# A two-layer attention trunk: the low parts of the mix weights come from an accumulating transfer instead of a VectorE subtraction

## The chip, the cores and the metric

One core of a Trainium2 chip runs the kernel. The metric is the device time of one execution in microseconds. A change counts as faster or slower when the time moves by more than 2%, which here is 13 us.

## The reference, cut to what matters

Two layers over 256 tokens of 1024 features. Each layer normalises, projects, runs three attention branches, gates each branch's product with `w_branch` by a sigmoid of its own mix columns, and projects the sum:

```
h = rmsnorm(x, norm_g)
proj = h @ w_in                       # ..., and 3 * 1024 mix columns at the end
ys = stack([ya, yb, ym])              # three branches, 512 wide each
up = einsum('bsnw,nwd->bsnd', ys, w_branch)
gates = sigmoid(mix.reshape(b, s, 3, 1024))
x = x + sum(gates * up, axis=2) @ w_out
```

Everything is float32. The kernel computes each float32 product as three products of rounded parts: a weight w is cut into a high part (`hi`, w rounded to the type float32r) and a low part (`lo` = w - `hi`), and the activations likewise.

## The kernel before, in words

Weights arrive in units. A unit is one transfer of up to 128 x 1024 floats from HBM into a tile `raw`, issued by SyncE (SP); ScalarE then copies `raw` into `whi` (line 102, shown as CAST), VectorE subtracts `whi` from `raw` into `wlo` (line 103), and TensorE multiplies. Units of the mix weights (`w_mix`) and of the branch weights (`w_br`) are 128 x 768, 384 KB. `mm3` (lines 106 to 108) issues three matmuls for a product: high by high, one with the activations' low part, one with the weights' low part. A mix unit and a branch unit have 18 matmuls each, of 256 columns; six of the 18 read `wlo`.

The tiles `raw`, `whi` and `wlo` have four buffers each, so a unit's parts can be written only after TensorE has finished with the unit four before it.

The order in each layer: memory branch, branch A, branch B (attention between `bq`, `bk`, `bv`), then the mix columns in eight groups j of 128 columns for the three branches. `mixes(j)` takes four mix units; the loop over j runs mixes three groups ahead, so its order is 16 mix units, then by turns two branch units and four mix units, then the last eight branch units, then `w_out`. For each j VectorE multiplies the gates into the branch products (line 543), GpSimd adds the three (lines 545 and 546), and ScalarE and VectorE split the sum (lines 547 and 548). A scheduler orders every engine's instructions by a model of its own; with it, matmuls of the first 16 mix units stand between those of branch B's attention. Each engine then runs its instructions in that order.

```python
def split(hi, lo, src):
    nc.scalar.copy(hi, src)
    nc.vector.tensor_sub(lo, src, hi.bitcast(F32))
```

Of the kernel before, what the change touches and what calls it, by code (L numbers as in the profile page):

```python
# [7 lines left out]
F32 = mybir.dt.float32  # L8
# [5 lines left out]
P = 128  # L14
D = 1024
S = 256
# [8 lines left out]
MS = 128 ** -0.5  # L25
RAW = 4  # units of weights on their way
WARM = 10  # products on zeros that wake the tensor engine's clock while the first loads are under way
WS = (64 ** -0.5) * (8 ** -0.5)

# columns of w_in, in groups of 512  # L30
A_Q, A_K, A_V, A_G, B_Q, B_K, B_V, B_G, M_Q, M_G = range(10)
# [3 lines left out]
def trunk(ctx, tc, x, x_t, mem, mem_t, consts, norm_g, gains, w_grp, w_idx, w_mix, w_kv, w_br, w_o, final_g, out):  # L35
# [13 lines left out]
    def two(tag="big"):  # L49
        """a tile for the high and the low parts: [P, 2, 1024]"""  # L50
        return big.tile([P, 2, 1024], F32R, tag="big", name=tag)
# [26 lines left out]
    def unit(src, n, pieces=1):  # L78
# [11 lines left out]
        return hi, lo  # L90

    newest = []
    between = []

    def load_after(dst, src):
        """a load that waits for the newest unit, so that it doesn't hold up the units before it"""
        nc.gpsimd.tensor_copy(dst.rearrange("p a b -> p (a b)")[:, 0:1] if len(dst.shape) > 2 else dst[:, 0:1],
                              newest[0][:, 0:1].bitcast(F32))
        nc.sync.dma_start(dst, src)
# [19 lines left out]
    def transpose_to(dst_fn, src, t):  # L119
        """[P, 1024] -> 8 blocks [128, P]; dst_fn(c, psum [P, 4, 128])"""  # L120
        for c in range(2):
            pt = bank(pst, "pt")
            for i in range(4):
                nc.tensor.transpose(pt[:, i * P:(i + 1) * P], src[:, (4 * c + i) * P:(4 * c + i + 1) * P], ident)
            dst_fn(c, pt.rearrange("p (a b) -> p a b", b=P))

    def rstd_row(rows, rs):
        """1 / rms of the tokens: on partitions in rs, and in a row, the same on all partitions"""
        pt = bank(pst, "pt")
        for t in range(NT):  # L130
            rstd_of(rows[t], wk.tile([P, D], F32, tag="h", name="sq", bufs=3), rs[t])
            diag = wk.tile([P, P], F32, tag="yf", name="diag")
            nc.vector.tensor_scalar(diag, ident, rs[t], None, op0=ALU.mult)
            nc.tensor.matmul(pt[:, t * P:(t + 1) * P], ones, diag, start=t == 0, stop=True, skip_group_check=True)
        return pt[:, :S]
# [4 lines left out]
    def mem_prep(l, mh, ml, ks):  # L140
        """mem but for 1 / rms, with features on partitions"""
        for k in ks:
            g = gm[:, 1, l, k:k + 1]
            nc.scalar.activation(mh[:, k, :], memT[:, k, :], AF.Copy, scale=g)
            nc.vector.scalar_tensor_tensor(ml[:, k, :], memT[:, k, :], g, mh[:, k, :].bitcast(F32),
                                           op0=ALU.mult, op1=ALU.subtract)
# [13 lines left out]
    def rows_first(wsrc, xh, xl, parts, n, done, ahead=lambda u: None, pools=None, first=False):  # L160
        """tokens on partitions: out[t][:, part] = x @ w, w [P, KC, n]"""
        pools = pools or [(pmm, "mm")] * NT
        acc = [[bank(*pools[t]) for _ in parts] for t in range(NT)]
        step = 2 if n <= 512 else 1
        for u in range(KC // step):
            ahead(u)
            hi, lo = unit(wsrc[:, step * u:step * (u + 1), :], step * n, 2 if first and u == 0 else 1)
            for kk in range(step):
                k = step * u + kk
                for t in range(NT):  # L170
                    for i, (a, b) in enumerate(parts):
                        mm3(acc[t][i][:, :b - a], xh[:, k, t * P:(t + 1) * P], xl[:, k, t * P:(t + 1) * P],
                            hi[:, kk * n + a:kk * n + b], lo[:, kk * n + a:kk * n + b], k == 0, k == KC - 1)
        for t in range(NT):
            for i in range(len(parts)):
                done(t, i, acc[t][i])

    def cols_first(wsrc, xh, xl, nt, done, ahead=lambda u: None):
        """columns on partitions: out[c] = (x @ w).T, w [P, KC, nt * 128]; done(pair of tiles, psum)"""
        n = nt * P  # L180
        acc = [bank(pmm, "mm") for _ in range((nt + 1) // 2)]
        step = 2
        for u in range(KC // step):
            ahead(u)
            hi, lo = unit(wsrc[:, step * u:step * (u + 1), :], step * n)
            for kk in range(step):
                k = step * u + kk
                for c in range(nt):
                    o = acc[c // 2][:, (c % 2) * S:(c % 2 + 1) * S]
                    w0 = kk * n + c * P  # L190
                    mm3(o, hi[:, w0:w0 + P], lo[:, w0:w0 + P], xh[:, k, :], xl[:, k, :],
                        k == 0 and c % 2 == 0, k == KC - 1)
        for c in range((nt + 1) // 2):
            done(c, acc[c])

    def rope(t, ps, dst, nh):
        """dst [P, nh, 64] = rope of psum [P, nh, 64]"""
        cb = cosv[t][:, None, :].to_broadcast([P, nh, 16])
# [10 lines left out]
    def heads_T(qf, dst):  # L209
        """qf[t] [P, 512] -> dst [P, 2, (pair, token)], heads on partitions"""  # L210
        for c in range(2):
            pt = bank(pst, "pt")
            for i in range(2):
                for t in range(NT):
                    j = 2 * c + i
                    nc.tensor.transpose(pt[:, i * S + t * P:i * S + (t + 1) * P], qf[t][:, j * P:(j + 1) * P], ident)  # L216
            split(dst[:, 0, c * 512:(c + 1) * 512], dst[:, 1, c * 512:(c + 1) * 512], pt)
# [11 lines left out]
    def values(l, g, hh, hl, name):  # L229
        """[P, token tile, (head, part, 64)]: the high part first for even heads, last for odd ones, so that it  # L230
        meets the rows of y that the head has"""
        v = two(name)
# [9 lines left out]
    def gate(l, g, hh, hl, s2):  # L242
        """s2 [P, 4, S] = 2 silu(h @ w).T"""
        def done(c, ps):
# [5 lines left out]
    def probs(t, nk, tm, nb, scale=-1.0):  # L250
        """softmax rows of scale * tm, whose maximum is -nb"""
        pr = wk.tile([P, 2, S], F32, tag="pr", name="pr", bufs=4)
# [10 lines left out]
    def pair_scores(p, qT, kT, at):  # L263
        """both heads of a pair, each on its half of the rows and in its own bank: queries of the first tile
        meet the high and the low parts of their 128 keys side by side, those of the second tile all keys"""
        scs = [bank(psa, "sc").rearrange("p (a b) -> p a b", b=S) for _ in range(2)]
# [29 lines left out]
    def attn_out(p, prs, v, y, s2):  # L296
# [13 lines left out]
        for i, pool in enumerate(((psa, "sc"), (pst, "pt"))):  # L310
            # high and low parts of v on rows; the low parts of the second queries' later keys in columns of their own
            yp = bank(*pool)
# [58 lines left out]
    def index_mask(l, hh, hl):  # L371
        """additive masks of the keys that each query picks"""
        qb = wk.tile([P, NT, 512], F32, tag="h", name="qf", bufs=3)
# [38 lines left out]
        def turn(t, r):  # L412
            """one turn of a query tile: takes the 8 largest that are left, the earlier of equals first"""
            nk = P * (t + 1)
# [15 lines left out]
    def normed_first(xT):  # L430
        """of x that is laid out with features on partitions"""
        hh = big.tile([P, KC, S], F32R, tag="big", name="hh")
# [22 lines left out]
    for l in range(L):  # L455
# [54 lines left out]
        def mixes(j):  # L510
            """tanh(mix / 2).T of columns j of the branches"""
            mx = wk.tile([P, 3, S], F32, tag="mix", name="mx", bufs=5)

            def done(c, ps):
                n = 2 if c == 0 else 1
                nc.scalar.activation(mx[:, 2 * c:2 * c + n, :], ps[:, :n * S].rearrange("p (a b) -> p a b", b=S),  # L516
                                     AF.Tanh, scale=0.5)
            cols_first(w_mix[l, j], hh, hl, 3, done)
            return mx
# [31 lines left out]
        last = 3 if l + 1 == L else 0  # L551
        # pieces of the columns of out, each in its own bank; the last ones small, as nothing runs beside their ends
        cuts = [[(0, 512), (512, 1024)], [(0, 512), (512, 768), (768, 1024)] if last else [(0, 512), (512, 1024)]]
# [52 lines left out]
def _constants():  # L606
    """identity, causal masks, cosines and sines: of the shapes alone"""
    import numpy as np
# [65 lines left out]
```

## Time and profile before

| | us |
|---|---|
| device time, median of 2 runs (647.31 and 647.63) | 647.47 |
| span of the profiled execution, first to last instruction | 645.5 |
| what lies around the span (the difference) | 2.0 |
| TensorE matmuls busy | 632.1 |
| VectorE busy | 468.8 |
| ScalarE busy | 372.6 |
| GpSimd busy | 121.0 |

The two runs differ by 0.05%. The profiled execution's own time is its span and some 2.0 us around it. Matmuls overlap, so TensorE's busy time says when it was supplied, not that each busy microsecond is a matmul's own; how far apart matmuls start says how fast it runs.

### The profile page before, as it was taken

The page shows a single profiled execution, that of the slowest core. Times are in us where ns is not written, and L with a number is a line of the kernel's source. Part 1 is how long each engine was busy: PE and PEld are TensorE (multiplying, and loading weights), DVE is VectorE, ACT ScalarE, POOL GpSimd, SP SyncE. Part 2 cuts the span into 40 slices and gives each one's busy share as a digit, 9 for nine tenths or more (in the row PEclk, how much of TensorE's full clock was granted, in tenths as well). Part 3 has the DMA queues.
Part 4 walks back from the last instruction along what each step waited for, and adds up shares of the span by engine and source line. Part 5 has one row for each costly group of instructions (what it writes and reads, how often), then busy time and mean ns, then how long its engine had stood idle before and what let it go on. Part 6 is the DMA issues. An engine that isn't in the chain of part 4 may idle for free.

```text
span 645.5 us, 12071 instructions
## 1 busy us (share of the span) xinstructions
PE 632.1 (98%) x4446; PEld 583.1 (90%) x4446; DVE 468.8 (73%) x1014; ACT 372.6 (58%) x725; POOL 121.0 (19%) x182
## 2 busy tenths in 40 slices
PE   7999999999999999999999999999999999999995
PEld 4989889878999999999889998897898999999984
DVE  5678799778777778557584678987777786755763
ACT  5857655666656756444464656656565766544442
POOL 1303022023102302126010200401210211221422
PEclk9999999999999999999999999999999999999998
DMA  8967454454444456667655745445444445566641
GB/s 298 360 201 233 150 160 141 156 162 137 111 142 124 125 145 198 195 174 221 214 174 135 264 152 164 134 133 170 151 127 133 131 127 148 171 187 184 206 127 65
DMA packets 35051, 108.64 MB, mean 168 GB/s; under 512 B 4016, under 2 KB 4016, under 8 KB 34992
## 3 DMA queue, kind: packets, MB, share of 16 engines
q1 hardware_dynamic: 34704, 107.35, 54.7%
q8 instruction: 35, 0.57, 0.4%
q10 hardware_dynamic: 288, 0.52, 0.2%
q14 instruction: 24, 0.20, 0.1%
HBM read 106.81 MB, written 1.05 MB: 167 GB/s over the span
## 4 chain that ended last, share of the span: by engine, by line
PE 93%; DMA 3%; DVE 2%; ACT 1%; issue 1%; SPq 0%; POOLq 0%; POOL 0%; ACTq 0%; DVEq 0%
PE mm L106 24%; PE mm L108 24%; PE mm L107 24%; PE sc L271 2%; PE sc L108 2%; PE sc L106 2%; PE sc L107 2%; DMA raw<-in_w_kv 2%; PE sc L275 2%; PE pt L216 1%; PE pt L301 1%; DMA xT<-in_x_t 1%; PE pt L106 1%; PE pt L108 1%; PE pt L107 1%; PE pt L303 1%
## 5 line engine op out<-in xcount | busy, mean ns | idle before, releaser
L103 DVE TENSOR_TENSOR wlo<-raw,whi 128x1024 fp32r<-128x1024 f32 (+3 forms) x225 | 246.9, 1099 | 99.5 <-ACT whi L102 98.5
L102 ACT CAST whi<-raw 128x1024 fp32r<-128x1024 f32 (+3 forms) x225 | 208.1, 927 | 130.3 <-PE mm L107 52.0
L107 PE MATMUL mm<-hl,whi 128*128 128x256 f32 x640 | 183.4, 287 | 0.0
L106 PE MATMUL mm<-hh,whi 128*128 128x256 f32 x640 | 182.9, 286 | 0.0
L108 PE MATMUL mm<-hh,wlo 128*128 128x256 f32 x640 | 182.6, 286 | 0.0
L106 PEld LDWEIGHTS mm<-hh,whi 128*128 128x128 f32 x640 | 122.6, 192 | 1.3
L107 PEld LDWEIGHTS mm<-hl,whi 128*128 128x128 f32 x640 | 122.6, 192 | 0.8
L108 PEld LDWEIGHTS mm<-hh,wlo 128*128 128x128 f32 x640 | 122.4, 192 | 0.7
L108 PE MATMUL mm<-whi,hl 128*128 128x512 f32 (+1 forms) x224 | 84.8, 381 | 1.4 <-DVE hl L103 1.4
L107 PE MATMUL mm<-wlo,hh 128*128 128x512 f32 (+1 forms) x224 | 85.7, 384 | 0.0
L106 PE MATMUL mm<-whi,hh 128*128 128x512 f32 (+1 forms) x224 | 84.2, 380 | 0.0
L260 POOL TENSOR_SCALAR pr<-pr,rinv 128x256 f32<-128x256 f32 (+1 forms) x80 | 40.7, 526 | 183.6 <-DVE rinv L258 175.9
L108 PEld LDWEIGHTS mm<-whi,hl 128*128 128x128 f32 x224 | 42.1, 189 | 8.3 <-DVE hl L103 1.7
L107 PEld LDWEIGHTS mm<-wlo,hh 128*128 128x128 f32 x224 | 42.2, 189 | 7.0
L106 PEld LDWEIGHTS mm<-whi,hh 128*128 128x128 f32 x224 | 41.8, 188 | 7.3
L255 ACT ACTIVATE pr<-tm,nb 128x128 f32<-128x128 f32 (+1 forms) x80 | 36.5, 459 | 9.1 <-DVE nb L291 9.0
L545 POOL TENSOR_TENSOR mx<-mx 128x256 f32<-128x256 f32 x16 | 21.3, 1334 | 102.8 <-DVE mx L543 102.8
L207 POOL TENSOR_TENSOR qf<-rt,rt 128x128 f32<-128x128 f32 (+2 forms) x24 | 16.8, 704 | 121.2 <-DVE rt L206 121.2
L546 POOL TENSOR_TENSOR mx<-mx 128x256 f32<-128x256 f32 x16 | 23.1, 1446 | 12.6 <-DVE mx L543 11.5
L543 DVE SCALAR_TENSOR_TENSOR mx<-mx,mm 128x256 f32<-128x256 f32 x48 | 18.6, 415 | 6.6 <-PE mm L108 6.5
L516 ACT ACTIVATE mx<-mm 128x512 f32<-128x512 f32 (+1 forms) x32 | 15.7, 490 | 12.9 <-PE mm L108 12.9
L547 ACT ACTIVATE mgh<-mx 128x256 fp32r<-128x256 f32 x16 | 6.7, 418 | 25.5 <-POOL mx L546 25.5
(252 smaller groups left out, 1220.9 us busy)
## 6 DMA issues: line engine op xcount, KB each, us to landing
raw<-in_w_grp SPq DMA_DIRECT2D x80, 512.0 KB, 3.9
raw<-in_w_mix SPq DMA_DIRECT2D x64, 384.0 KB, 3.2
raw<-in_w_br SPq DMA_DIRECT2D x32, 384.0 KB, 3.4
raw<-in_w_o SPq DMA_DIRECT2D x16, 512.0 KB, 4.4
raw<-in_w_kv SPq DMA_DIRECT2D x15, 512.0 KB, 4.4
raw<-in_w_idx SPq DMA_DIRECT2D x16, 292.0 KB, 3.1
memT<-in_mem_t SPq DMA_DIRECT2D x4, 256.0 KB, 6.0
xr<-in_x SPq DMA_DIRECT2D x2, 512.0 KB, 6.6
```

The lines of the kernel that those rows point to most:

```text
L102: nc.scalar.copy(hi, src)
L103: nc.vector.tensor_sub(lo, src, hi.bitcast(F32))
L106: nc.tensor.matmul(o, lh, rh, start=start, stop=False, skip_group_check=True)
L107: nc.tensor.matmul(o, lh, rl, start=False, stop=False, skip_group_check=True)
L108: nc.tensor.matmul(o, ll, rh, start=False, stop=stop, skip_group_check=True)
L207: nc.gpsimd.tensor_tensor(dst[:, :, 0:16], t1[:, :nh], t2[:, :nh], op=ALU.add)
L255: nc.scalar.activation(pr[:, i, :nk], tm[:, i, :nk], AF.Exp, bias=nb[:, i:i + 1], scale=scale, accum_out=rsum[:, i:i + 1])
L260: nc.gpsimd.tensor_scalar(pr[:, i, :nk], pr[:, i, :nk], rinv[:, i:i + 1], 1.0, op0=ALU.mult, op1=ALU.mult)
L516: nc.scalar.activation(mx[:, 2 * c:2 * c + n, :], ps[:, :n * S].rearrange("p (a b) -> p a b", b=S), AF.Tanh, scale=0.5)
L543: nc.vector.scalar_tensor_tensor(mt[n], mx[:, n, :], 1.0, ups[n // 2][:, (n % 2) * S:(n % 2 + 1) * S], op0=ALU.add, op1=ALU.mult)
L545: nc.gpsimd.tensor_tensor(mt[0], mt[0], mt[1], op=ALU.add)
L546: nc.gpsimd.tensor_tensor(mt[0], mt[0], mt[2], op=ALU.add)
```

## The change

The mix units, and no others, get their parts in another way (`unit_sum`). ScalarE copies `raw` into `whi` as before, then writes `-whi` into `wlo` by an activation with scale -1; then GpSimd issues a transfer that reads the same 384 KB of `w_mix` from HBM a second time and adds it onto `wlo`. VectorE's subtraction of those units is gone. The sum is the same: `-hi + w`. The other lines of the diff only remove comments, which moves line numbers by up to 14.

```diff
+    def unit_sum(src, n):
+
+        raw = wp.tile([P, 1024], F32, tag="raw", name="raw", bufs=RAW)
+        hi = wp.tile([P, 1024], F32R, tag="whi", name="whi")
+        lo = wp.tile([P, 1024], F32R, tag="wlo", name="wlo")
+        nc.sync.dma_start(raw[:, :n], src)
+        nc.scalar.copy(hi[:, :n], raw[:, :n])
+        nc.scalar.activation(lo[:, :n], hi[:, :n].bitcast(F32), AF.Copy, scale=-1.0)
+        nc.gpsimd.dma_start(lo[:, :n].rearrange("p (a b) -> p a b", b=384), src, accum_op=ALU.add)
+        newest[:] = [lo]
+        if between:
+            between.pop(0)()
+        return hi, lo
...
-    def cols_first(wsrc, xh, xl, nt, done, ahead=lambda u: None):
+    def cols_first(wsrc, xh, xl, nt, done, ahead=lambda u: None, get=None):
...
-            hi, lo = unit(wsrc[:, step * u:step * (u + 1), :], step * n)
+            hi, lo = (get or unit)(wsrc[:, step * u:step * (u + 1), :], step * n)
...
-            cols_first(w_mix[l, j], hh, hl, 3, done)
+            cols_first(w_mix[l, j], hh, hl, 3, done, get=unit_sum)
```

There are 64 mix units, 32 a layer, so 64 subtractions go and 64 activations and 64 GpSimd transfers come. The scheduler also orders the engines anew. In the rows below a number behind a name is a buffer's; a low part has the number of its high part and one more.

TensorE in the first layer, before, where the third and the fourth mix unit of `mixes(5)` meet (`whi_3287`, `whi_3311`): the matmuls of a unit stand together, and its low part is read in its third matmul.

```order
L107 MATMUL mm_3237<-hl_323,whi_3287 128x256
L108 MATMUL mm_3237<-hh_322,wlo_3288 128x256
L106 MATMUL mm_3236<-hh_322,whi_3311 128x256
L107 MATMUL mm_3236<-hl_323,whi_3311 128x256
L108 MATMUL mm_3236<-hh_322,wlo_3312 128x256
L106 MATMUL mm_3236<-hh_322,whi_3311 128x256
```

The same place now, where the third mix unit of `mixes(5)` begins (`whi_3309`, low part `wlo_3310`) and a branch unit (`whi_3363`, low part `wlo_3364`) comes into it:

```order
L120 MATMUL mm_3256<-hh_322,whi_3309 128x256
L121 MATMUL mm_3256<-hl_323,whi_3309 128x256
L120 MATMUL mm_3257<-hh_322,whi_3309 128x256
L121 MATMUL mm_3257<-hl_323,whi_3309 128x256
L122 MATMUL mm_3360<-yA_1542,wlo_3364 128x256
L120 MATMUL mm_3360<-yA_1542,whi_3363 128x256
L121 MATMUL mm_3360<-yA_1542,whi_3363 128x256
L122 MATMUL mm_3360<-yA_1542,wlo_3364 128x256
```

Four matmuls of the mix unit that need no low part come first, then the remaining 16 of the branch unit, and the mix unit's other 14 only after those; so this mix unit ends 16 matmuls later, and its buffers come free that much closer to the unit that takes them next.

ScalarE at that place, before:

```order
L102 CAST whi_3287<-raw_3286 128x768
L102 CAST whi_3311<-raw_3310 128x768
L102 CAST whi_3339<-raw_3338 128x768
L547 ACTIVATE mgh_2614<-mx_2717 128x256
L102 CAST whi_3363<-raw_3362 128x768
L102 CAST whi_3397<-raw_3396 128x768
```

And now, from the branch units (`whi_3363`, `whi_3387`) to the first mix units of `mixes(6)`:

```order
L116 CAST whi_3363<-raw_3362 128x768
L116 CAST whi_3387<-raw_3386 128x768
L98 CAST whi_3421<-raw_3420 128x768
L99 ACTIVATE wlo_3422<-whi_3421 128x768
L98 CAST whi_3446<-raw_3445 128x768
L99 ACTIVATE wlo_3447<-whi_3446 128x768
```

Each mix unit has two instructions of the same size on ScalarE now.

GpSimd in the first layer, before, from the last softmax rows (`pr`) of branch B to the sums of the gated products (`mx`) of j = 0 and j = 1:

```order
L260 TENSOR_SCALAR pr_2540<-pr_2540,rinv_2544 128x256 x2
L545 TENSOR_TENSOR mx_2616<-mx_2616 128x256
L546 TENSOR_TENSOR mx_2616<-mx_2616 128x256
L545 TENSOR_TENSOR mx_2717<-mx_2717 128x256
L546 TENSOR_TENSOR mx_2717<-mx_2717 128x256
```

And now, from the second mix unit of `mixes(4)` to that of `mixes(5)`:

```order
L100 DMA wlo_3123<-in_w_mix 128x768
L559 TENSOR_TENSOR mx_2616<-mx_2616 128x256
L100 DMA wlo_3148<-in_w_mix 128x768
L100 DMA wlo_3173<-in_w_mix 128x768
L560 TENSOR_TENSOR mx_2616<-mx_2616 128x256
L100 DMA wlo_3260<-in_w_mix 128x768
L559 TENSOR_TENSOR mx_2721<-mx_2721 128x256
L560 TENSOR_TENSOR mx_2721<-mx_2721 128x256
L100 DMA wlo_3285<-in_w_mix 128x768
```

Transfers stand between the sums, and `wlo_3285`'s stands behind both sums of j = 1.

## Rows read from the trace of the kernel before

**Rows 1.** The page: engines' busy time, and the chain that ended last.

```profile
PE 632.1 (98%) x4446; PEld 583.1 (90%) x4446; DVE 468.8 (73%) x1014; ACT 372.6 (58%) x725; POOL 121.0 (19%) x182
...
PE 93%; DMA 3%; DVE 2%; ACT 1%; issue 1%; SPq 0%; POOLq 0%; POOL 0%; ACTq 0%; DVEq 0%
```

**Rows 2.** Waits of TensorE's matmuls, whole span: us in total, times, longest.

```profile
PE mm L106 <- ACT whi L102: 2.1, 2, 1.2
PE pt L74 <- POOL idle L71: 1.5, 1, 1.5
PE mm L108 <- DVE hl L103: 1.4, 1, 1.4
PE mm L107 <- DVE wlo L103: 0.5, 1, 0.5
```

**Rows 3.** Timeline of TensorE among mix units: start us, us, what.

```profile
257.06 0.28 PE L107 MATMUL mm<-hl,whi 128*128 128x256 f32 x1
257.18 0.28 PE L108 MATMUL mm<-hh,wlo 128*128 128x256 f32 x1
257.30 0.28 PE L106 MATMUL mm<-hh,whi 128*128 128x256 f32 x1
```

**Rows 4.** Busy time by stretch; first layer's attention with mix, mix with branch units.

```profile
core 0: us, PE busy (x) PEld busy (x) DVE busy (x) ACT busy (x) POOL busy (x), PEclk, DMA share, GB/s
189.00:232.00 43.00, 43.00 (x354) 41.41 (x353) 33.86 (x93) 28.16 (x72) 8.13 (x16) 1.00 0.50 138
...
258.00:271.00 13.00, 13.00 (x111) 13.00 (x110) 7.21 (x11) 6.08 (x9) 2.84 (x2) 1.00 0.67 189
```

**Rows 5.** Groups by line within 189 to 232 us: busy us, mean ns, idle before.

```profile
L103 DVE TENSOR_TENSOR wlo<-raw,whi 128x768 fp32r<-128x768 f32 x16 | 15.6, 975 | 5.0 <-ACT whi L102 5.0
L102 ACT CAST whi<-raw 128x768 fp32r<-128x768 f32 x15 | 12.5, 831 | 4.8 <-PE mm L107 2.8 <-ACT yf L319 0.9 <-ACT pr L255 0.7
```

**Rows 6.** Timeline of ScalarE among mix and branch units, with idle time before.

```profile
267.46 0.83 ACT L102 CAST whi<-raw 128x768 fp32r<-128x768 f32 x1 [0.72 <-PE mm L107]
269.62 0.83 ACT L102 CAST whi<-raw 128x768 fp32r<-128x768 f32 x1 [1.33 <-PE mm L107]
```

**Rows 7.** Timeline of VectorE, the same place.

```profile
268.33 0.96 DVE L103 TENSOR_TENSOR wlo<-raw,whi 128x768 fp32r<-128x768 f32 x1 [0.59 <-ACT whi L102]
270.49 0.96 DVE L103 TENSOR_TENSOR wlo<-raw,whi 128x768 fp32r<-128x768 f32 x1 [1.20 <-ACT whi L102]
```

**Rows 8.** The page's transfers, whole span: KB each, median us from issue to landing.

```profile
raw<-in_w_grp SPq DMA_DIRECT2D x80, 512.0 KB, 3.9
raw<-in_w_mix SPq DMA_DIRECT2D x64, 384.0 KB, 3.2
```

**Rows 9.** Transfers within 10 to 26 us: queue's MB and share, then landings.

```profile
q1 hardware_dynamic: 2081, 6.58, 102.2%
...
raw<-in_w_idx SPq DMA_DIRECT2D x3, 292.0 KB, 5.3
xr<-in_x SPq DMA_DIRECT2D x2, 512.0 KB, 6.6
```

**Rows 10.** GpSimd's shortest compute instruction: ns least, median, most.

```profile
L348 POOL TENSOR_SCALAR nb<-mx x8: 213/218/248, 87.6 to 409.2; 128x2 f32<-128x2 f32 x8
```

**Rows 11.** Timeline of GpSimd among mix and branch units.

```profile
262.66 1.39 POOL L545 TENSOR_TENSOR mx<-mx 128x256 f32<-128x256 f32 x1 [9.82 <-DVE mx L543]
264.12 1.45 POOL L546 TENSOR_TENSOR mx<-mx 128x256 f32<-128x256 f32 x1
```

**Rows 12.** VectorE's gating by line 543: ns least, median, most.

```profile
L543 DVE SCALAR_TENSOR_TENSOR mx<-mx,mm x48: 405/415/424, 236.3 to 616.9; 128x256 f32<-128x256 f32 x48
```

## The prediction

> **What bounds the kernel now.** I read the page first: TensorE's matmuls are busy 98% of the span, and 93% of the chain that ended last is TensorE [rows 1]. VectorE, which the change relieves, is busy 73% and holds 2% of the chain. The next view is what TensorE's matmuls waited for: all entries together are 5.5 us, and the one on a VectorE low part is a single 0.5 us [rows 2]. The reader should see that VectorE delivers in time nearly everywhere. Third, the timeline: matmuls start 0.12 us apart [rows 3] at a granted clock of 1.00, and in the stretch of mix and branch units TensorE is busy 13 of 13 us [rows 4]. So a mix unit of 18 matmuls takes 2.16 us, and six units 13 us.
>
> Supply is what the change touches, and four buffers set it. ScalarE's copies there start when TensorE releases the unit four before (267.46 and 269.62 us, 2.16 apart, released by PE) [rows 6], and VectorE's subtraction follows 0.04 us after the copy's end, ending at 269.29 [rows 7]. So release to finished low part is 0.83 + 0.04 + 0.96 = 1.8 us. In the order before, the first matmul on a low part stands 57 matmuls, 6.8 us, behind the last one of the unit four before it: 5 us of slack.
>
> **The change part by part.**
>
> *Removed:* 64 subtractions of 0.975 us [rows 5], 62 us of VectorE. On the path they are worth nothing, because TensorE hardly waited for them; the most that could come back is the 0.5 us of [rows 2]. Bound: a gain of 0 to 0.5 us; I take 0.
>
> *Added on ScalarE:* 64 activations of 128 x 768. The copy of that size takes 0.83 us [rows 5, 6], and I take the same. That is 53 us in all. With mix and branch units ScalarE goes from 6.1 to 9.4 of 13 us, beside TensorE. In branch B's attention it goes from 28.2 to 28.2 + 16 x 0.83 = 41.4 of 43 us [rows 4]: costed at nothing as work of its own, with the first 4.8 us of waits before copies [rows 5] as its cover, and a rival below if that cover fails.
>
> *Added on GpSimd and the transfer queues:* 64 transfers that add. The trace has none, so both parts are bounded. Issue: between GpSimd's shortest instruction, 0.22 us [rows 10], and its longer sums, 1.45 us [rows 11]; I take the middle, 0.9, since writing out a transfer is neither. Landing: at least that of the plain load of the same weights, 3.2 us [rows 8]. But the transfer must read `wlo` as well as HBM, 768 KB for 384. From 384 to 512 KB a landing grows from 3.2 to 3.9 us [rows 8], 0.7 per 128 KB, so 384 KB more cost 2.1: 5.3 us, my value. At a full queue (102% share) 292 and 512 KB land in 5.3 and 6.6 us [rows 9], 0.6 per 100 KB, which carried on to 768 KB gives 8.1, the upper end.
>
> The Trainium skill, "DMA: Bandwidth & Descriptors", section on latency, gives about 1 us to the first byte of a transfer that GpSimd issues and about 0.6 for SyncE's; with 1.0 as the issue the sum below would be some 1 us longer. No run so far shows it.
>
> *The new chain.* From release to a usable low part: copy 0.83, activation 0.83, issue 0.9, landing 5.3, handovers 0.1; 8.0 us instead of 1.8. Bounds: 5.2 (0.22 and 3.2) and 11.3 (1.45 and 8.1).
>
> *What covers it, and where it doesn't.* The cover is the work that TensorE has between release and first use, 0.12 us a matmul, counted in the changed order. The scheduler pulls branch matmuls forward there, so several mix units end 16 matmuls later and their successors have 39 to 41 matmuls of cover, 4.7 to 4.9 us, where they had 57. First layer, the stall where 8.0 exceeds the cover (a unit that shares a stall already paid only adds the rest): first two mix units, 56 and 53 matmuls: 1.3 and 0.4. The other 14 units of the attention stretch have 71 to 88 matmuls, 8.5 us or more: 0. Then, for units of `mixes(4)` to `mixes(7)`, 63, 50 and 39: 0.4, 1.6, 3.3; 41: 3.1; 39: 3.3; 39: 3.3. Sum 16.7 us. Second layer: 1.3, 0.4, 0.4, 1.6, 3.3 (39), 3.3 (39), 3.8 (35), 1.3 (56), 1.3 (45): 16.7 too.
>
> *GpSimd's queue.* It runs in order, and in the first layer the transfer for the second unit of `mixes(5)` stands behind both sums of j = 1. Those need the branch unit's products, a gating of 0.42 us [rows 12], then 1.39 and 1.45 us [rows 11]; I take 2 us of delay there, once (0 to 3), since other transfers behind a sum have longer cover. SyncE's order of loads is unchanged, and their raw buffers come free no later.
>
> *Sum:* 2 x 16.7 + 2 = 35 us. The profiled execution's 645.5 us of span plus 2.0 around it becomes 680.9 + 2.0, **683 us**; 647.5 is the median also, so nothing else is adjusted. With the bounds of the chain: at 5.2 us only the covers of 35 to 41 matmuls are short, by 0.3 to 1.0 each, 4 us in all: **651**. At 11.3 us the attention stretch is short too (some 12 us a layer), and the six short places cost 31: 43 a layer, 2 for the queue, **736**.
>
> **The rivals.**
>
> *Hidden anyway (not slower).* The transfer lands like the plain load and is issued in 0.2 us; chain 5.2 us, decided at 6.0 us, below which the sum stays under 13. Time 651. For it: the 3.2 us landing is of the same bytes from HBM [rows 8]. Against: two reads, and a queue that is already 0.67 busy [rows 4].
>
> *The transfer engines become the bound.* Six loads of 13 us take a share of 0.67, 0.112 each [rows 4]. Count each added transfer as two loads: 14 x 0.112 = 1.56, so 13 us become 20.3, four turns a layer: +29. In the attention stretch 16 loads take 0.50; with 32 more it is 1.50, 43 us become 64.5: +21.5. Both layers: +101, **748**. For it: the shares. Against: a share counts waiting too. At 10 to 26 us, 6.58 MB went in 16 us, 411 GB/s [rows 9], and at that rate 14 loads of 0.393 MB need 13.4 us and the attention stretch's 48 need 45.9, only 4.5 us a layer too many, inside the stalls already counted. It decides if adding runs well below the plain rate.
> The Trainium skill, "Collectives: The Full Stack", part 3 on the bandwidth ceiling, says of an adding transfer that "the add needs **two source reads**" on one ring, so that it moves half as fast as a copy. By it this rival's count of two is right, and the truth lies between 683 and 748; the trace of before has no such transfer.
>
> *ScalarE becomes the bound beside attention.* At 41.4 of 43 us any wait that stays pushes the softmax and the copies behind it. If none of ScalarE's 14.8 us of idle time there can be filled, each layer's stretch grows by 13.3, on top of 15 from the later places: 2 x 28.3 + 2 = +59, **706**. For it: in-order waits on TensorE's releases are real [rows 6]. Against: softmax also waits for VectorE, which has 16 us less to do.
>
> *Faster.* Nothing on the path is removed; I leave it 1%.
>
> **How the numbers follow.** Forecast (683, from 660 to 705 for chains of 6 to 9.5 us) 0.51; hidden 0.16; transfer engines 0.20; ScalarE 0.12; faster 0.01. The predicted time is the forecast's. The range runs from 653 to 745: it leaves out most of the hidden case and the upper part of the transfer case, some 0.2 together. The measurement tells about 2%, 13 us, from no change. Faster 0.01; within 2%: the hidden case and the forecast's low end, 0.19; slower 0.80.
>
> **What would show it.** In the changed profile TensorE should wait for `wlo` in pieces of 1 to 4 us, some six to nine places a layer, mostly where branch units alternate with mix units and little during attention; the wait's releaser should be the transfer. The landing of the adding transfers should be near 5.3 us. VectorE should lose 62 us and the span gain. I am wrong on the low side if landings are near 3 us; on the high side if the share of the transfer engines stands at 1.0 through the whole mix stretch, if GpSimd holds each issue for well over 1.5 us, or if the granted clock drops below 1.00 after the new stalls, which the trace of before, with its full supply, can't show.

## The result and the profile after

The changed kernel takes 713.74 us (median of 2 runs, 711.78 to 715.70) where the kernel before takes 647.47. The ratio is 1.1027, with an interval of 1.0995 to 1.106: slower, by 66 us.

The page of the changed kernel, the lines that answer to [rows 1], [rows 5] and [rows 8]: busy time, the granted clock in tenths over 40 slices, two transfer queues (packets, MB, share; q1 is SyncE's, q0 GpSimd's), the chain that ended last, three groups by line, three transfers with KB and landing.

```profile
PE 652.5 (92%) x4446; PEld 598.8 (84%) x4446; DVE 410.9 (58%) x950; ACT 420.9 (59%) x789; POOL 167.6 (24%) x246
...
PEclk9999999999999999899999999999999999998999
...
q1 hardware_dynamic: 34704, 107.35, 48.0%
q0 software_dynamic: 9216, 25.17, 20.2%
...
PE 68%; DMA 17%; issue 7%; DVE 3%; ACT 2%; POOL 1%; SPq 0%; POOLq 0%; DVEq 0%; ACTq 0%
...
L122 PE MATMUL mm<-hh,wlo 128*128 128x256 f32 x640 | 184.9, 299 | 45.8 <-DMA wlo<-in_w_mix 45.7
...
L100 POOL DMA_DIRECT2D wlo<-in_w_mix x64 | 57.0, 898 | 156.2 <-ACT wlo L99 110.0
...
L99 ACT ACTIVATE wlo<-whi 128x768 fp32r<-128x768 f32 x64 | 53.6, 842 | 0.8
...
raw<-in_w_mix SPq DMA_DIRECT2D x64, 384.0 KB, 5.2
wlo<-in_w_mix POOLq DMA_DIRECT2D x64, 384.0 KB, 7.4
raw<-in_w_br SPq DMA_DIRECT2D x32, 384.0 KB, 4.3
```

What the reader is to see: TensorE runs the same 4446 matmuls, its share of the span falls from 98% to 92%, and a transfer has come into the chain that ended last, with 17%. VectorE gave up 58 us (468.8 to 410.9) and nothing came of it. The span grew from 645.5 to 710.0 us, by 64.5, and it divides in two. TensorE's idle time went from 13.4 us (645.5 - 632.1) to 57.5 (710.0 - 652.5): 44.1 more. Its busy time for the same matmuls went from 632.1 to 652.5: 20.4 more, most of it the clock's, as the windows below show.

What TensorE's matmuls waited for, the answer to [rows 2] (us in total, times, longest): the wait on the adding transfer is larger than the whole growth of the idle time.

```profile
PE mm L122 <- DMA wlo<-in_w_mix: 45.7, 19, 4.7
PE pt L74 <- POOL idle L71: 1.5, 1, 1.5
```

One of these waits, link by link. TensorE's timeline (start, us, what, idle time before in brackets), with ScalarE's and GpSimd's rows for the same unit:

```profile
284.36 0.28 PE L121 MATMUL mm<-hl,whi 128*128 128x256 f32 x1
288.50 0.58 PE L122 MATMUL mm<-hh,wlo 128*128 128x256 f32 x1 [3.87 <-DMA wlo<-in_w_mix]
288.88 0.42 PE L120 MATMUL mm<-hh,whi 128*128 128x256 f32 x1
289.10 0.41 PE L121 MATMUL mm<-hl,whi 128*128 128x256 f32 x1
```

```profile
278.32 0.83 ACT L98 CAST whi<-raw 128x768 fp32r<-128x768 f32 x1 [1.57 <-PE mm L121]
279.18 0.85 ACT L99 ACTIVATE wlo<-whi 128x768 fp32r<-128x768 f32 x1
```

```profile
280.43 0.88 POOL L100 DMA_DIRECT2D wlo<-in_w_mix  x1 [9.52 <-ACT wlo L99]
```

The chain of work that ended last, there (start, us, what):

```profile
280.43 8.03 DMA wlo<-in_w_mix
288.46 0.04 issue
```

TensorE frees a buffer at 278.3. The copy takes 0.86 us to the next start, the negation 0.85, then 0.40 pass before GpSimd begins the transfer, which lands 8.03 us after that beginning (GpSimd's 0.88 us of issue are in it): 10.2 us from release to a usable low part. (Over all 64 units the median is 10.9 us, worked out with the buffers' addresses in the built program.) TensorE had 6.3 us of work meanwhile (278.3 to 284.6) and then stood 3.87 us. Behind the wait its matmuls start 0.21 us apart, where [rows 3] show 0.12.

The stretches of [rows 4], with the same columns (us, busy time of PE, PEld, DVE, ACT, POOL, granted clock, DMA share, GB/s), and 3 us behind six of the waits:

```profile
core 0: us, PE busy (x) PEld busy (x) DVE busy (x) ACT busy (x) POOL busy (x), PEclk, DMA share, GB/s
176.00:238.00 62.00, 55.16 (x402) 51.10 (x401) 26.30 (x88) 45.48 (x98) 21.00 (x32) 0.97 0.94 221
262.00:290.00 28.00, 19.27 (x138) 18.54 (x137) 6.24 (x13) 16.22 (x25) 10.11 (x12) 0.88 0.89 214
290.00:312.00 22.00, 18.28 (x128) 18.07 (x128) 3.51 (x6) 10.14 (x14) 5.06 (x6) 0.84 0.91 214
...
196.60:199.60 3.00, 2.98 (x19) 2.73 (x20) 1.51 (x10) 0.76 (x3) 0.93 (x2) 0.73 1.07 282
236.50:239.50 3.00, 3.00 (x25) 3.00 (x26) 0.83 (x3) 1.14 (x2) 0.00 (x0) 1.00 0.51 202
252.00:255.00 3.00, 2.95 (x16) 2.98 (x17) 0.00 (x0) 0.25 (x1) 0.00 (x0) 0.60 1.06 268
269.80:272.80 3.00, 3.00 (x14) 3.00 (x15) 0.00 (x0) 0.00 (x0) 0.89 (x1) 0.50 1.10 299
288.50:291.50 3.00, 3.00 (x14) 3.00 (x15) 0.00 (x0) 0.00 (x0) 0.90 (x1) 0.50 1.06 269
543.40:546.40 3.00, 3.00 (x25) 2.73 (x26) 1.71 (x10) 1.00 (x3) 0.94 (x2) 1.00 1.05 263
```

The waits that end at 196.62, 252.05, 269.77 and 288.50 lasted 3.08, 3.95, 4.66 and 3.87 us, and behind each the granted clock is 0.50 to 0.73: it is at its lower level, 1.2 GHz, or on its way there, and 14 to 19 matmuls fit in 3 us. Those that end at 236.47 and 543.37 lasted 2.13 and 2.50 us, and the clock stays at 1.00 (2.4 GHz) with 25 matmuls in 3 us. The DMA share is 0.89 to 0.94 through whole stretches, where [rows 4] have 0.50 and 0.67.

### The profile page after: what moved, and what is told of

Its sections match the earlier page's. It is cut to its first block, busy times and chain, and to the rows that moved or that the text cites. A ratio compares the mean times of both kernels' runs of the same rounds, so it can differ in the third digit from the quotient of the medians.

```text
span 710.0 us, 12223 instructions
## 1 busy us (share of the span) xinstructions
PE 652.5 (92%) x4446; PEld 598.8 (84%) x4446; DVE 410.9 (58%) x950; ACT 420.9 (59%) x789; POOL 167.6 (24%) x246
## 3 DMA queue, kind: packets, MB, share of 16 engines
q0 software_dynamic: 9216, 25.17, 20.2%
## 4 chain that ended last, share of the span: by engine, by line
PE 68%; DMA 17%; issue 7%; DVE 3%; ACT 2%; POOL 1%; SPq 0%; POOLq 0%; DVEq 0%; ACTq 0%
PE mm L122 18%; PE mm L121 18%; PE mm L120 17%; DMA wlo<-in_w_mix 15%; PE sc L120 2%; PE sc L121 2%; PE sc L122 2%; PE sc L285 2%; PE sc L289 1%; PE pt L230 1%; PE pt L120 1%; PE pt L315 1%; PE pt L122 1%; PE pt L121 1%; DVE wlo L117 1%
## 5 line engine op out<-in xcount | busy, mean ns | idle before, releaser
L117 DVE TENSOR_TENSOR wlo<-raw,whi 128x1024 fp32r<-128x1024 f32 (+3 forms) x161 | 184.3, 1147 | 114.2 <-ACT whi L116 111.8
L116 ACT CAST whi<-raw 128x1024 fp32r<-128x1024 f32 (+3 forms) x161 | 155.1, 965 | 145.6 <-PE mm L121 79.5
L122 PE MATMUL mm<-hh,wlo 128*128 128x256 f32 x640 | 184.9, 299 | 45.8 <-DMA wlo<-in_w_mix 45.7
L121 PE MATMUL mm<-hl,whi 128*128 128x256 f32 x640 | 187.4, 296 | 0.0
L120 PE MATMUL mm<-hh,whi 128*128 128x256 f32 x640 | 186.3, 294 | 0.0
L121 PEld LDWEIGHTS mm<-hl,whi 128*128 128x128 f32 x640 | 129.2, 202 | 1.3
L120 PEld LDWEIGHTS mm<-hh,whi 128*128 128x128 f32 x640 | 129.2, 202 | 0.9
L100 POOL DMA_DIRECT2D wlo<-in_w_mix x64 | 57.0, 898 | 156.2 <-ACT wlo L99 110.0
L98 ACT CAST whi<-raw 128x768 fp32r<-128x768 f32 x64 | 53.2, 831 | 22.2 <-PE mm L121 17.5
L99 ACT ACTIVATE wlo<-whi 128x768 fp32r<-128x768 f32 x64 | 53.6, 842 | 0.8
L559 POOL TENSOR_TENSOR mx<-mx 128x256 f32<-128x256 f32 x16 | 18.8, 1174 | 44.3 <-DVE mx L557 44.3
```

Source lines behind the costliest of these rows:

```text
L98: nc.scalar.copy(hi[:, :n], raw[:, :n])
L99: nc.scalar.activation(lo[:, :n], hi[:, :n].bitcast(F32), AF.Copy, scale=-1.0)
L100: nc.gpsimd.dma_start(lo[:, :n].rearrange("p (a b) -> p a b", b=384), src, accum_op=ALU.add)
L120: nc.tensor.matmul(o, lh, rh, start=start, stop=False, skip_group_check=True)
L121: nc.tensor.matmul(o, lh, rl, start=False, stop=False, skip_group_check=True)
L122: nc.tensor.matmul(o, ll, rh, start=False, stop=stop, skip_group_check=True)
```

## The experiments

The theory: the chain from a freed buffer to a usable low part has become longer than the work that four buffers hold, so TensorE stands, and its clock falls on top of it. The rivals: the transfer engines (twice the bytes for the low parts, whoever waits for them), ScalarE beside attention, and the adding itself. Differences are against the kernel before on the same chip (646.8 to 647.4 us).

**1. The negation from the loaded tile, the same transfers (e4).** The negation is taken from `raw`, and the program names it ahead of the copy (line 98 is the negation here and line 99 the copy).

```diff
+        nc.scalar.activation(lo[:, :n], raw[:, :n], AF.Copy, scale=-1.0)
         nc.scalar.copy(hi[:, :n], raw[:, :n])
-        nc.scalar.activation(lo[:, :n], hi[:, :n].bitcast(F32), AF.Copy, scale=-1.0)
```

> ScalarE writes the negated rounded weight straight from the loaded tile and before it writes the high part, so the adding transfer starts one ScalarE instruction, 0.83 us, earlier; the same values. Chain theory: 0.83 us less in each of some 9 stalls a layer and less time at the low clock, 695 to 704 us. Traffic theory: within 5 us of 714.

Measured: 693.26 us, ratio 1.0717 (1.0686 to 1.0748), 46 us over before instead of 66, 2 us below the range of the chain theory. The landing is 7.4 us as in the changed kernel. But the edit did not take one link out of every chain: the scheduler ordered ScalarE anew, and the negation stands ahead of the copy in the first four mix units of each layer alone. In the other 56 the copy is still first, as here:

```profile
251.10 0.83 ACT L99 CAST whi<-raw 128x768 fp32r<-128x768 f32 x1 [1.88 <-PE mm L121]
251.84 0.84 ACT L98 ACTIVATE wlo<-raw 128x768 fp32r<-128x768 f32 x1
```

So the 20 us are not the price of a link of 0.85 us. Where the new order did shorten the chain, the waits went: for the units of `mixes(0)` to `mixes(3)` the time from a low part's release to the start of its transfer fell from 3.3 to 2.0 us in the median (worked out with the buffers' addresses), and TensorE's waits for these transfers from 12.5 to 1.8 us. For the other units that time stayed at 2.4 us, and the waits went from 33.2 to 29.0 us. The cover in matmuls is nearly the same in both kernels (medians 74.5 and 74.5, 60 and 61.5). That is latency against cover, at unchanged bytes and landing; a bound of the transfer engines would not give it.

**2. One buffer fewer, in both kernels (e9, e10).**

```diff
-    wp = ctx.enter_context(tc.tile_pool(name="wp", bufs=4))
+    wp = ctx.enter_context(tc.tile_pool(name="wp", bufs=3))
```

> The changed kernel with three buffers for the high and low parts instead of four. Chain theory: one unit less of cover, 2.2 us, in the order that it gets; stalls counted for a chain of 8.7 us rise from 44 to 88 us, and with the low clock behind them the time is 765 to 800 us. Traffic theory: the bytes are the same, within 15 us of 714.

> The kernel before the change with three buffers for the high and low parts. Chain theory: two units of cover are 4.3 us, the chain by VectorE is 1.8 us, so 647 to 655 us. If three buffers cost by themselves, for another reason, it is slower than 660.

Measured: the changed kernel 750.74 us, ratio 1.1602 (1.1564 to 1.164); the kernel before 648.26, ratio 1.0013 (0.9997 to 1.0028). The same buffer is worth 37 us to the one and at most 2 us to the other. TensorE's wait on the transfer with three buffers:

```profile
PE mm L122 <- DMA wlo<-in_w_mix: 69.9, 29, 5.6
```

29 waits instead of 19. Both have an order of their own. The direction is that of the chain, the size below what I expected; a landing of 6.3 instead of 7.4 us may give some of it back.

**3. One buffer more for the low parts (e8).** The edit of e4, and `wlo` with five buffers (in both functions that load units); the room comes from `mx`, which goes from five to four.

```diff
-        lo = wp.tile([P, 1024], F32R, tag="wlo", name="wlo")
+        lo = wp.tile([P, 1024], F32R, tag="wlo", name="wlo", bufs=5)
...
-            mx = wk.tile([P, 3, S], F32, tag="mix", name="mx", bufs=5)
+            mx = wk.tile([P, 3, S], F32, tag="mix", name="mx", bufs=4)
```

> Low parts have five buffers instead of four (room comes from one buffer less for the gates), and ScalarE writes the negated rounded weight first and straight from the loaded tile. All 64 adding transfers stay, with the same bytes; the values are the same. Chain theory: the matmuls between the release of a low part's buffer and the first matmul on the next unit in it grow to 75 or more nearly everywhere, 9 us, against a chain of 0.84 + 7.4 = 8.2 us; stalls of 2 to 5 us in all, granted clock 0.99, time 648 to 656 us, level with the kernel before. Traffic theory: the bytes and the share of the transfer engines are those of the change, so 690 us or more.

Measured: 668.03 us, ratio 1.0333 (1.0306 to 1.036). Of the change's 66 us 46 come back, 25 more than in e4, with the same 25.17 MB of adding transfers and a landing of 7.5 us. The 25 us are not the buffer's alone: here the negation does stand ahead of the copy, in 63 of the 64 units. The cover grows from 60 to 76 matmuls in the median behind attention. I had expected nearly all of the 66 us back, and 21 stayed. Its stretches:

```profile
core 0: us, PE busy (x) PEld busy (x) DVE busy (x) ACT busy (x) POOL busy (x), PEclk, DMA share, GB/s
196.00:238.00 42.00, 41.30 (x332) 39.76 (x331) 19.20 (x64) 34.62 (x75) 17.49 (x26) 1.00 1.02 255
262.00:290.00 28.00, 26.24 (x213) 25.55 (x213) 6.93 (x12) 17.39 (x27) 9.98 (x12) 1.00 1.01 265
```

With the waits shorter the same bytes go in less time and the share reaches 1.01 to 1.02. TensorE still waits 12.1 us for the transfer. Whether the full engines or the long landing keep that up, this run doesn't say.

**4. The same without the adding (e11).**

```diff
-        nc.gpsimd.dma_start(lo[:, :n].rearrange("p (a b) -> p a b", b=384), src, accum_op=ALU.add)
+        nc.gpsimd.dma_start(lo[:, :n].rearrange("p (a b) -> p a b", b=384), src)
```

> The version with five low parts and the negation first, with a plain transfer from GpSimd instead of the adding one: the low part is the whole weight, so the result is not the reference's. If what is left over there (668 us, 20 over the kernel before, transfer engines at a share of 1.0 through the mix stretch) is the second read of the addition, the share falls to 0.85 or less and the time to 647 to 653 us. If it is ScalarE's added work or GpSimd's queue, the time stays at 660 or more.

Measured: 652.58 us, ratio 1.0081 (1.0066 to 1.0096); 15 of the 21 us went. Every engine has the order of e8, so the 15 us are the adding's; the landing falls with it, from 7.5 to 4.8 us, so that engine time and a shorter chain can't be told apart here. The lines of its page on GpSimd's queue and transfer:

```profile
q0 software_dynamic: 9216, 25.17, 13.1%
...
L100 POOL DMA_DIRECT2D wlo<-in_w_mix x64 | 35.6, 556 | 145.0 <-ACT wlo L98 83.1
...
wlo<-in_w_mix POOLq DMA_DIRECT2D x64, 384.0 KB, 4.8
```

The same stretches have a share of 0.85 and 0.87 here, and TensorE is busy 42.00 and 27.22 us of 42 and 28. Over the span GpSimd's queue holds the engines for 0.131 x 650.8 = 85 us; in e8 its share is 20.4%, 0.204 x 663.8 = 135 us, for the same 25.17 MB. Adding costs 1.6 times the engine time of copying.

**5. The changed kernel without the adding, and adding from SBUF (e2, e5).** e2 makes the edit of e11 alone, with four buffers. e5 keeps the adding and takes the other operand from a tile in SBUF, so that the weights are read from HBM once:

```diff
-        nc.gpsimd.dma_start(lo[:, :n].rearrange("p (a b) -> p a b", b=384), src, accum_op=ALU.add)
+        nc.gpsimd.dma_start(lo[:, :n], hh[:, 0:3, :].rearrange("p a b -> p (a b)").bitcast(F32), accum_op=ALU.add)
```

> The transfer no longer adds: GpSimd copies w_mix onto the low part, so the low part is the whole weight and the result is not the reference's. Everything else stays. If the addition (a second read) makes the landing long, the landing falls from 7.4 to some 4.5 to 5.5 us and the time to 665 to 690 us. If the way by GpSimd makes it long, or the queueing behind other loads, the landing stays near 7 and the time within 1.5% of 714 us.

> The adding transfer reads its addend from the activations' tile in SBUF instead of from HBM, so the low part is wrong, and the second read of w_mix from HBM is left out. If HBM's bandwidth or latency makes the landing long, it falls to 5.5 us or less and the time to 690 us or less. If it is the two reads and the write in the transfer engines themselves, the landing stays at 6.5 us or more and the time at 700 to 716.

Measured: e2 682.89 us, ratio 1.0556 (1.0519 to 1.0593); e5 689.43, ratio 1.0657 (1.0627 to 1.0688). For e5 the answer is mixed: the landing is that of the second case, the time that of the first. The pages, e2's and then e5's:

```profile
q0 software_dynamic: 9216, 25.17, 13.2%
...
wlo<-in_w_mix POOLq DMA_DIRECT2D x64, 384.0 KB, 4.6
```

```profile
q0 software_dynamic: 9216, 25.17, 19.9%
...
wlo<-hh POOLq DMA_DIRECT2D x64, 384.0 KB, 6.5
```

A copy by GpSimd lands in 4.6 us, adding from SBUF in 6.5, adding from HBM in 7.4. So adding instead of copying from HBM costs 2.8 us of landing, and an addend in SBUF saves 0.9 of it. Both versions keep the changed kernel's order on every engine, so these are the plainest tests of the chain: in e5 a landing 0.9 us shorter, at nearly the same time of the transfer engines (0.199 x 687.1 = 137 us, where the changed kernel has 0.202 x 710.0 = 143), takes the waits on the transfer from 45.7 to 30.3 us and gives back 24 us. (The loads of the mix units land in 5.0 us there, where the changed kernel has 5.2, so a relief of HBM's reads hardly shows in them.) Even the copy leaves TensorE 21.1 us of waiting and the kernel 36 us slower: the way over a transfer was too long for four buffers without any adding. The Trainium skill, "Collectives: The Full Stack", part 3 on the bandwidth ceiling, says of the add in a ReduceScatter that it needs two source reads and moves half as fast as a copy; the runs agree in direction (13.2 against 19.9 and 20.2%), with 1.6 in place of 2.

**6. The traffic alone (e1, e1b, e1c).** VectorE subtracts as before, and GpSimd adds the weights onto a spare tile that nobody reads.

```diff
-        nc.scalar.activation(lo[:, :n], hi[:, :n].bitcast(F32), AF.Copy, scale=-1.0)
-        nc.gpsimd.dma_start(lo[:, :n].rearrange("p (a b) -> p a b", b=384), src, accum_op=ALU.add)
+        nc.vector.tensor_sub(lo[:, :n], raw[:, :n], hi[:, :n].bitcast(F32))
+        dm = wk.tile([P, D], F32, tag="h", name="dm", bufs=3)
+        nc.gpsimd.memset(dm[:, :n], 0.0)
+        nc.gpsimd.tensor_copy(dm[:, 0:1], hi[:, 0:1].bitcast(F32))
+        nc.gpsimd.dma_start(dm[:, :n].rearrange("p (a b) -> p a b", b=384), src, accum_op=ALU.add)
```

> Leaves nothing out of the result: VectorE subtracts the mix units' low parts as before the change, and beside it GpSimd zeroes a spare tile and issues the same adding transfer of w_mix onto it, tied to the unit's high part; no other engine waits for it. So the extra traffic and GpSimd's issues stay, and the long chain is off the path. Chain theory (what costs is the time from a buffer's release to a usable low part, against the work that four buffers leave TensorE): 646 to 656 us, TensorE's waits for low parts under 4 us, granted clock 0.99. Traffic theory (the transfer engines are full, and loads and additions queue for them): 680 us or more, with TensorE or ScalarE waiting for loads.

Measured: 721.17 us, ratio 1.1148 (1.111 to 1.1186). It tells nothing of traffic, since I had made a new wait. From its waits:

```profile
POOL dm L101 <- DMA dm<-in_w_mix: 125.6, 52, 6.6
...
ACT mgh L564 <- POOL mx L563: 72.0, 14, 10.6
```

GpSimd stands 125.6 us for the spare tile's last transfer, and the softmax scalings and the sums of the mixes stand behind it in its queue. e1b mends that: the scalings (`probs`) and the sums go to VectorE, and the copy of one column is gone. e1c is the kernel before with only those moves.

```diff
-            nc.gpsimd.tensor_scalar(pr[:, i, :nk], pr[:, i, :nk], rinv[:, i:i + 1], 1.0, op0=ALU.mult, op1=ALU.mult)
+            nc.vector.tensor_scalar(pr[:, i, :nk], pr[:, i, :nk], rinv[:, i:i + 1], 1.0, op0=ALU.mult, op1=ALU.mult)
...
-            nc.gpsimd.tensor_tensor(mt[0], mt[0], mt[1], op=ALU.add)
+            nc.vector.tensor_tensor(mt[0], mt[0], mt[1], op=ALU.add)
```

> The traffic beside the work once more, with nothing else on GpSimd that others wait for: VectorE subtracts the low parts as before, and also scales the softmax rows and adds the gated products; GpSimd only zeroes spare tiles and issues the 64 adding transfers onto them. Chain theory: 647 to 660 us. Traffic theory: 680 or more, with waits for loads.

> The kernel before the change with softmax scaling and the gated sums on VectorE instead of GpSimd, as in the second run of the traffic beside the work (658 us), and without that traffic. If the traffic costs what that run lost, this one takes 646 to 650 us; if moving the work to VectorE does, 655 to 659.

Measured: e1b 658.08 us, ratio 1.017 (1.0149 to 1.019); e1c 647.25, ratio 1.0001 (0.9991 to 1.0011). All other engines have the same order in both. 64 adding transfers that nothing on the path waits for cost 11 us (e1b also has 64 memsets on GpSimd, which e1c doesn't have, so they are in this figure). The way it costs is in e1b's landings of the plain loads:

```profile
dm<-in_w_mix POOLq DMA_DIRECT2D x64, 384.0 KB, 7.7
raw<-in_w_mix SPq DMA_DIRECT2D x64, 384.0 KB, 6.7
raw<-in_w_br SPq DMA_DIRECT2D x32, 384.0 KB, 6.2
```

`raw` takes 6.7 us where it took 3.2 [rows 8], and ScalarE's copies of the mix units wait 28.1 us for it in all.

**7. Which half of the units (e6, e7).** The transfer adds only for `mixes(0)` to `mixes(3)`, which run beside attention, or only for the other four; the rest goes by VectorE as before.

```diff
-            cols_first(w_mix[l, j], hh, hl, 3, done, get=unit_sum)
+            cols_first(w_mix[l, j], hh, hl, 3, done, get=unit_sum if j < 4 else None)
```

(e7 has `if j > 3`.)

> Adding transfers for the first four column groups alone, the 16 mix units a layer that stand among branch B's attention; the other 16 get VectorE's subtraction. Chain theory: only the first two units have less than 8.5 us of cover (57 and 54 matmuls), some 6 to 13 us of stalls in both layers and 2 to 5 us of low clock, 655 to 666 us. If ScalarE, at 41 of 43 us there by the prediction's count, is a bound of its own: 675 or more.

> Adding transfers for the last four column groups alone, the 16 mix units a layer that alternate with branch units. Chain theory: 33 us of stalls in both layers by the order it gets and a chain of 8.7 us, and some 15 us of low clock behind them, 690 to 700 us. The costs of the two halves should add up to the change's 66 us within 10. Traffic theory, by bytes: half of the change's cost, 680.

Measured: e6 663.10 us, ratio 1.0248 (1.0228 to 1.0269); e7 690.12, ratio 1.0666 (1.0645 to 1.0687). 16 and 43 us, 59 of the 66 (each version has an order of its own). Nearly three quarters of the 59 lie where mix and branch units alternate, as both theory and prediction had it. e6 leaves little room for ScalarE as a bound of its own beside attention: the rival asked 27 us there (2 x 13.3), and the waits that e6 shows are on the transfer (9.5 us), not on ScalarE (1.3 us). ScalarE's queue does stand in the chain ahead of those transfers, as the next section shows.

No version came below the kernel before, and there was little to gain: TensorE is busy 98% of its span [rows 1].

## Why the prediction was right, and where it was off

**The direction and the mechanism held.** 713.74 against 683, inside the range. VectorE's relief was worth nothing; ScalarE's activation took 0.842 us (0.83 said), GpSimd's issue 0.898 (0.9 said, where the middle of its two bounds is 0.84); TensorE waits for `wlo` at 19 places, nine or ten a layer (six to nine said), with the transfer as releaser, most and longest where branch units alternate. e5, e8, e9 and e10 show the chain and its cover as the main cause: a landing 0.9 us shorter gives back 24 us, a fifth buffer with the negation first 46, a buffer less costs 37, and a buffer less does nothing to the kernel before.

The Trainium skill, "DMA: Bandwidth & Descriptors", section on latency, has about 1 us to the first byte of a transfer that GpSimd issues. The trace has more: of ten added transfers that start with no other under way, the first packet of GpSimd's queue starts 1.6 to 3.3 us after the issue's start, 1.74 in the median.

**The landing was mis-sized.** "Issue 0.9 + landing 5.3" is 6.2 us; the transfers landed in 7.4 in the median, counted from the start of the issue, and in 8.03 at the place shown. The prediction had added bytes by the growth from 384 to 512 KB. For the second operand's bytes it had 2.1 us; adding instead of copying takes 2.8 (e2), and the plain copy by GpSimd already lands in 4.6 and not in 3.2. The plain loads beside it are later too (`raw` of the mix units 5.2 instead of 3.2). The handover from ScalarE to GpSimd, in the 0.1 us for all of them, was 0.40. At that place the chain is 10.2 us and not 8.0.

**The cover was mis-counted, the other way.** The prediction set a unit against the one four before it and got 39 matmuls, 4.7 us, for the unit that stands at 288.50. The trace shows its copy starting at 278.32, right behind the last matmul of a branch unit on a high part; the mix unit four before it has 14 matmuls left that start from 278.24 to 279.80:

```profile
278.00 0.28 PE L121 MATMUL mm<-yM,whi 128*128 128x256 f32 x1
278.12 0.28 PE L122 MATMUL mm<-yM,wlo 128*128 128x256 f32 x1
278.24 0.28 PE L122 MATMUL mm<-hh,wlo 128*128 128x256 f32 x1
...
279.80 0.28 PE L122 MATMUL mm<-hh,wlo 128*128 128x256 f32 x1
```

So it can't have taken that unit's buffer; it took the branch unit's, which came free first, and the cover was 6.3 us, 52 matmuls. The two errors nearly cancel, which is luck: 8.0 - 4.7 is 3.3, and 10.2 - 6.3 is 3.9. The addresses in the built program show the same at every place that the prediction counted at 35 to 41 matmuls: 52 to 63. Nor is it the new order that makes covers short: by addresses, the order before has 56 or 58 matmuls, some 7 us, at 26 of the 32 later units, less than a chain of 10 us needs.

**The stalls in sum:** 35 us said, 44.1 measured. Told by the unit that is waited for, the waits on the transfer are 33.2 us for `mixes(4)` to `mixes(7)` of both layers, where the prediction had 30, and 12.5 us for `mixes(0)` to `mixes(3)`, beside attention, where it had 3.4. In the first layer the latter are 3.08, 0.31, 0.53, 0.79 and 2.13 us, all at units that it had put at nothing, and none at the two units that it had named. The 2 us for GpSimd's queue can't be told apart from these.

What was missed beside attention is ScalarE's queue, which the prediction had costed at nothing. Other copies and the softmax stand in it, so that the time from a release to the start of GpSimd's transfer is 3.3 us in the median there, against 2.4 for the later units, and a usable low part comes 10.9 us after its release, behind the 8.5 us or more of cover that were to hide it. The same queue makes the longest wait of all; its timeline:

```profile
258.58 0.82 ACT L98 CAST whi<-raw 128x768 fp32r<-128x768 f32 x1
259.30 3.30 ACT L158 ACTIVATE mh<-memT,gm 128x256 fp32r<-128x256 f32 x8
262.51 0.83 ACT L99 ACTIVATE wlo<-whi 128x768 fp32r<-128x768 f32 x1
```

Eight activations of the memory branch (L158) stand between the copy and its negation, which begins 3 us later for it; the wait that this chain ends, at 269.77 with 4.66 us, is the longest of all. In order of issue an added instruction costs what stands ahead of it too.

**The term that was missing is the clock.** The prediction named "if the granted clock drops below 1.00 after the new stalls" as what would put it wrong on the high side and gave it nothing in the sum. It dropped at every wait of 3.08 us or more. In the stretches at 0.50 behind these nine waits TensorE is busy 32.7 us and starts 150 matmuls, which at 0.12 us each take 18.0: the lower clock cost some 15 us. The other 6 of the 20.4 us of busy time are not the clock. About half of them may be that a matmul ahead of a wait counts its whole 0.28 us and not 0.12 (20 more such waits); the rest stays open. 683 + 9 (stalls) + 15 (clock) + 6 (the rest) is 713; 713.74 was measured.

**The rivals.** *Hidden anyway* asked for a chain below 6.0 us; it was 10.2 at the place shown, and even the plain copy of e2 is 36 us slower. *The transfer engines* are a real second cause and not the first: the share stands near 0.9 through the mix stretch, close to the 1.0 that the prediction had named as this rival's sign, but traffic alone is 11 us (e1b against e1c), not 101. The adding, its longer landing included, is 15 us with five buffers (e8 against e11) and 31 with four (the changed kernel against e2). What the share of 0.9 couldn't say is how much TensorE loses by it. *ScalarE* was busy 45.5 of the 62 us from 176 to 238, where the prediction had 41.4 of 43; e6 speaks against it as a bound of its own, while its queue lengthens the chain there. The causes don't add up: they share the same waits, and e6 and e7 alone leave 7 us of the 66.

## What to carry to other kernels

Before an engine's step is handed to a transfer, set the whole chain from a freed buffer to usable data (every handover, the landing under the new traffic) against the work that the buffers hold, and count that work from the release in the trace, since buffers may come free in another order than they were made. Where a scheduler orders the engines, look up in the order that was built whether an edit moved what it was to move. If the bottleneck will stand for some microseconds at many places, add what its clock loses behind each. An engine that is busy 73% off the path is no reason to move its work onto a longer way.

## What the hardware showed that I had not expected

The clock falls behind quite short stalls. In this run the nine waits of 3.08 to 4.66 us for `wlo` were each followed by 3 us at a granted clock of 0.50 to 0.73, and the ten others, of 0.17 to 2.50 us, by 3 us at 1.00. At the lower level matmuls start 0.21 us apart, and 14 to 23 of them started at it behind each of the nine.

GpSimd holds an adding transfer for 0.898 us and a plain one of the same size for 0.556 (e11), a third of a microsecond more. Adding takes 1.6 times the engine time of the same copy (135 against 85 us), though its bytes in the profile are the same 25.17 MB: a queue's MB don't tell what it asks of the engines, its share does.
